# Queue order fixed by a walk over the traced program, and a fourth step by seven products per gate/up group, in a two-layer float32 decoder trunk

## The chip, the cores and the metric

The kernel runs on one core of a Trainium2 chip. The metric is the device time of one execution in microseconds (us). The kernel before takes 1836.91 us, the median of three runs (1836.82 to 1837.41).

## What is computed

The input is one sequence of 256 tokens with 2048 channels in float32, and it passes through two layers. Layer 0 mixes tokens by causal trailing means over windows of 2, 4, 8 and 16 tokens, one window for each quarter of the channels, followed by a 512 x 512 product per quarter. Layer 1 mixes tokens by differential attention with 8 heads. Each layer ends with a SwiGLU feed-forward block of width 5632. A root-mean-square norm stands before every block and at the end.

```python
def diff_attention(h, w_qkv, ...):
    qkv = h @ w_qkv                      # 2048 x 6144
    ...
    a = p[:, :, 0] - lam * p[:, :, 1]    # difference of two softmaxes, head by head
    ...
    return o.reshape(B, S, H * e) @ w_o  # 2048 x 2048

def swiglu(h, wg, wu, wd):               # 2048 x 5632, 2048 x 5632, 5632 x 2048
    return (jax.nn.silu(h @ wg) * (h @ wu)) @ wd

def reference(x, ...):
    h = x
    for i in range(DEPTH):               # DEPTH = 2
        mix = pool_mixer(rmsnorm(h), ...) if i % 2 == 0 else diff_attention(rmsnorm(h), ...)
        h = h + mix
        h = h + swiglu(rmsnorm(h, norm_ffn[i]), w_gate[i], w_up[i], w_down[i])
    return rmsnorm(h, final_norm)
```

## The kernel before

**The products.** Each float32 operand is split into a high and a low part of type float32r (`hi` by a cast, `lo` by subtracting it), and a product is the sum of three matmuls: high by high, high by low, low by high (line 187). The weights are the moving operand, 512 columns wide, and the activations the stationary one, 128 x 128.

`group` (line 147) makes one output block of 256 tokens by 1024 columns. It runs over steps of 256 input channels; a gate/up, q/k, v, o or a full down group has 8 steps. A step's weights come as one load of four blocks of 128 x 512 (`load`, line 116, 1 MiB on the SyncE queue). A step is multiplied in one of two ways:

- plain (line 156): eight block products, two into each of four PSUM banks C11, C12, C21, C22, that is 24 matmuls. It needs `halves` (line 121) of four blocks: a cast on ScalarE (line 124) and a subtraction on VectorE (line 125).
- by seven (line 153): seven block products in the manner of Strassen and Winograd, 21 matmuls, one block product into each of seven banks. It needs sums of the weight blocks (`sums`, line 128, three additions on VectorE at lines 130, 132, 133, written to `tsum`), the halves of these sums (`sum_halves`, line 136: `thi` by a cast on ScalarE at line 139, `tlo` by a subtraction on VectorE at line 140), and the halves of three blocks only.

All eight PSUM banks belong to a group (line 144). Banks 0 to 3 hold M1, M6, M7 and P5, which only steps by seven write; banks 4 to 7 hold P3, P4, M2 and X, which plain steps write under the names C12, C21, C11 and C22. `combined` (line 204) puts the results together with eight additions on VectorE and two copies on ScalarE. Transposes and the attention's small products borrow banks 0 to 3 in turn (`aux`, line 83).

**The stages.** The start (to line 436) loads the tokens and computes layer 0's mixer. `ffn` (line 466) works in chunks of 4, 4 and 3 gate/up groups (`CHUNKS`); each gate/up group gives two `h` tiles through `pair` (line 254), which transposes on TensorE and splits on ScalarE and VectorE; the chunk then runs two down groups with 8, 8 or 6 steps. The attention runs four q/k groups (line 596), each followed by two heads (`head`, line 566, whose scores at line 576, softmax at lines 578 to 592 and transposes at line 561 borrow banks 0 to 3), then two v groups (line 616) and two o groups (line 636).

**Which steps go by seven** is written down in tuples (lines 41 to 47). Gate/up: steps 2, 4, 6, and 4, 6 in the first group of a layer (line 482). Down: 2, 4, 6. The first q/k and the first v group: 4, 6 in natural order. The other q/k and v groups (`LATE`): the order 0, 1, 3, 5, 4, 2, 6, 7, with 4, 2, 6 by seven. An operand for a step by seven is held as eight blocks instead of four (`pair_shape`, line 102).

**Buffers.** Three raw weights (`wraw`), three pairs `whi`, `wlo` (`whl`), one `tsum`; one pair `thi`, `tlo` in the feed-forward blocks, two pairs in q, k, v and o (`bufs=2`).

**What sets the order.** Instructions are traced in the order of the program text. A scheduler of the language then orders each engine's queue from its own cost estimates and priorities; two stretches of the start are given a lower priority (lines 429 and 432). Each engine works through its queue in order and waits on semaphores.

Of the kernel before, what the change touches and what calls it, by code (L numbers as in the profile page):

```python
# [2 lines left out]

# [11 lines left out]
PSUM = bass.MemoryType.PSUM  # L15
# [5 lines left out]
NP = NK // 2  # L21
# [4 lines left out]
EPS = 1e-6  # L26
WARM = 8
LATER = 70

WINDOWS = (2, 4, 8, 16)  # L30

# [6 lines left out]
CHUNKS = (4, 4, 3)  # L38


SEVEN = (2, 4, 6)
SEVEN_DOWN = (2, 4, 6)
SEVEN_QKV = (2, 4, 6)

EARLY = (tuple(range(NP)), (4, 6))
LATE = ((0, 1, 3, 5, 4, 2, 6, 7), SEVEN_QKV)
SEVEN_O = (4, 6)


# [1 line left out]

A22, A21, A11, A12, S1, S3, S2, S4 = range(8)
T1, T3, T2, T4 = range(4)


@with_exitstack
def trunk_kernel(ctx, tc, x_n, gains, scale_in, final_in, subln, lam_in, band, counts_in, dist,
# [408 lines left out]
    def ffn(layer, xq, ss, next_op, next_gain):  # L466
# [3 lines left out]
        with tc.tile_pool(name=f"ffn{layer}", bufs=1, reuse_waits="tile") as hp:  # L470
            g0 = 0
            ys = []
            for c, n in enumerate(CHUNKS):
# [5 lines left out]
                        nc.scalar.dma_start(out=final_sb[i], in_=final_in[:, i * 1024:(i + 1) * 1024])  # L479
                for g in range(g0, g0 + n):  # L480

                    by_seven = SEVEN if g else SEVEN[1:]
                    cs = combined(group([(xq[p], p in by_seven, w_gu[layer][g, p]) for p in range(NP)], hp), hp)
                    for t in range(2):
                        gate, up = cs[t]
                        nc.scalar.activation(gate, gate, AF.Silu, scale=r[:, t:t + 1])
                        nc.vector.scalar_tensor_tensor(up, up, r[:, t:t + 1], gate, ALU.mult, ALU.mult)
                    for i in range(2):
                        at = 2 * (g - g0) + i
                        ht = hp.tile(pair_shape(at in SEVEN_DOWN), F32R, name="h", tag=f"h{at}")  # L490
                        pair(ht, lambda k, t: cs[t][1][:, (2 * i + k) * P:(2 * i + k + 1) * P], None, at in SEVEN_DOWN)
                        hp_tiles.append(ht)
# [35 lines left out]
    with tc.tile_pool(name="attn", bufs=1, reuse_waits="tile") as ap_, ExitStack() as heads:  # L528
# [86 lines left out]
        oT = [None] * NP  # L615
        for g in range(2):
            order, by_seven = LATE if g else EARLY
            cs = scaled(combined(group([(xp[p], p in by_seven, w_v[g, p]) for p in order], op_, bufs=2), op_), (r_col, r_col))
            for h in range(4 * g, 4 * g + 4):
                v = [cs[t][h % 4 // 2][:, h % 2 * E:(h % 2 + 1) * E] for t in range(2)]  # L620
                op = aux((P, 2, E))
# [12 lines left out]
                pair(oT[h], lambda i, t: on[:, t, i * P:(i + 1) * P], [gs[:, i:i + 1] for i in range(2)], h in SEVEN_O)  # L634
        xq = operand(SEVEN)
        for g in range(2):
            cs = combined(group([(oT[p], p in SEVEN_O, w_o[g, p]) for p in range(NP)], op_, bufs=2), op_)
            for b in range(2):
                j = 2 * g + b
                for t in range(2):  # L640
# [2 lines left out]
                transposed(xq, j, 4, SEVEN)  # L643

    ffn(1, xq, ss_next, None, None)


def _steps(w, left, right):
# [85 lines left out]
```

## Time and profile before

| What | Value |
| --- | --- |
| median of three runs | 1836.91 us |
| profiled execution, in all | 1837.09 us |
| its span, first to last instruction | 1835.3 us |
| granted TensorE clock | 0.998 of full speed |
| ScalarE busy | 1048.7 us (57%) |
| memory traffic | 356.35 MB, mean 194 GB/s |
| weight load, issue to landing | 4.8 us median for 1 MiB |

In the profile PE is TensorE's matmuls and PEld its weight loads (which overlap), DVE is VectorE, ACT is ScalarE, SP is SyncE, which issues the large loads. L189 is line 189 of the kernel. `b<-whi,xp` means that a PSUM bank is written from `whi` and `xp`. A group row has the count behind an x, then busy us and the mean ns of one, then the engine's idle time just before these instructions and what ended most of it. A timeline row has the start and the duration in us.

### The profile page before, as it was taken

Reading aid. Unit: us, or ns where it says so; the run is one execution under the profiler, and the core shown is the slowest. Engines: PE = TensorE matmul, PEld = TensorE weight load, DVE = VectorE, ACT = ScalarE, POOL = GpSimd, SP = SyncE. Lnnn points to the kernel's source line nnn. Section 1 sums busy time; section 2 is a strip of 40 time slices with the busy share of each in tenths; the row PEclk is TensorE's granted clock in tenths of the full one; section 3 lists DMA queues with packets and bytes.
Section 4 is the critical chain, followed back from the end, with each engine's and each line's share of the span. In section 5 each row is a group of like instructions: output and inputs, shape, how many; then the busy total and the mean of one; then the engine's idle time right before and its main releaser. Section 6 shows DMA issues by size and latency. Waiting matters only on the chain.

```text
span 1835.3 us, 20926 instructions
## 1 busy us (share of the span) xinstructions
PE 1823.0 (99%) x8192; PEld 1492.3 (81%) x8192; DVE 1630.5 (89%) x1692; ACT 1048.7 (57%) x1026; POOL 0.7 (0%) x6
## 2 busy tenths in 40 slices
PE   9999999999999999999999999999999999999997
PEld 6888888888888888888888888888888888888886
DVE  7999999889899899989988789889899899988986
ACT  6655544555554556666667665555554555555563
POOL 0000000000000000000000000000000000000000
PEclk9999999999999999999999999999999999999999
DMA  7555555555555555544554555555555545556552
GB/s 271 200 184 193 208 196 209 204 187 205 205 194 197 205 184 184 206 173 174 182 183 163 181 184 184 206 185 205 204 190 202 207 183 193 212 215 210 202 189 110
DMA packets 50930, 356.35 MB, mean 194 GB/s; under 512 B 6160, under 2 KB 6288, under 8 KB 8464
## 3 DMA queue, kind: packets, MB, share of 16 engines
q1 hardware_dynamic: 49968, 353.40, 53.5%
q10 hardware_dynamic: 864, 1.63, 0.2%
q8 instruction: 64, 1.05, 0.2%
q14 instruction: 34, 0.28, 0.0%
HBM read 352.90 MB, written 2.10 MB: 193 GB/s over the span
## 4 chain that ended last, share of the span: by engine, by line
PE 97%; DVE 1%; ACT 1%; DMA 0%; issue 0%; SPq 0%; DVEq 0%; ACTq 0%
PE b L189 93%; PE b L259 2%; PE b L576 1%; PE b L607 0%; DMA x_tok<-x_n 0%; PE b L368 0%; PE b L624 0%; PE b L622 0%; PE b L623 0%; PE b L561 0%; DVE wlo L354 0%; DVE xt_hl L252 0%; ACT sq L240 0%; DVE wlo L125 0%; DVE z L392 0%
## 5 line engine op out<-in xcount | busy, mean ns | idle before, releaser
L189 PE MATMUL b<-whi,xp 128*128 128x512 f32 x2784 | 899.4, 392 | 0.0
L124 ACT CAST whi<-raw 128x1536 fp32r<-128x1536 f32 (+1 forms) x328 | 578.7, 1764 | 549.6 <-PE b L189 450.4
L125 DVE TENSOR_TENSOR wlo<-raw,whi 128x1536 fp32r<-128x1536 f32 (+1 forms) x328 | 689.6, 2103 | 159.2 <-ACT whi L124 158.9
L189 PEld LDWEIGHTS b<-whi,xp 128*128 128x128 f32 x2784 | 520.1, 188 | 108.2 <-ACT e L272 0.4
L189 PE MATMUL b<-wlo,xp 128*128 128x512 f32 x1392 | 544.2, 391 | 0.0
L189 PE MATMUL b<-whi,h 128*128 128x512 f32 x1108 | 354.2, 390 | 0.0
L189 PEld LDWEIGHTS b<-wlo,xp 128*128 128x128 f32 x1392 | 261.5, 188 | 53.0
L140 DVE TENSOR_TENSOR tlo<-tsum,thi 128x2048 fp32r<-128x2048 f32 x114 | 260.6, 2286 | 8.3 <-ACT thi L139 8.3
L189 PEld LDWEIGHTS b<-whi,h 128*128 128x128 f32 x1108 | 207.5, 188 | 43.2
L139 ACT CAST thi<-tsum 128x2048 fp32r<-128x2048 f32 x114 | 217.6, 1908 | 19.7 <-DVE tsum L133 17.2
L189 PE MATMUL b<-thi,xp 128*128 128x512 f32 x640 | 223.4, 389 | 0.0
L189 PE MATMUL b<-wlo,h 128*128 128x512 f32 x554 | 215.8, 389 | 0.0
L130 DVE TENSOR_TENSOR tsum<-raw 128x1024 f32<-128x1024 f32 x114 | 139.1, 1220 | 2.1 <-DMA raw<-w_v 0.6
L189 PEld LDWEIGHTS b<-thi,xp 128*128 128x128 f32 x640 | 120.1, 188 | 24.7
L189 PE MATMUL b<-tlo,xp 128*128 128x512 f32 x320 | 125.9, 393 | 0.0
L189 PEld LDWEIGHTS b<-wlo,h 128*128 128x128 f32 x554 | 104.0, 188 | 21.3
L189 PE MATMUL b<-thi,h 128*128 128x512 f32 x240 | 83.7, 390 | 0.0
L133 DVE TENSOR_TENSOR tsum<-tsum,raw 128x512 f32<-128x512 f32 x114 | 78.5, 689 | 2.2
L132 DVE TENSOR_TENSOR tsum<-tsum,raw 128x512 f32<-128x512 f32 x114 | 78.1, 685 | 0.6
L189 PEld LDWEIGHTS b<-tlo,xp 128*128 128x128 f32 x320 | 60.0, 188 | 16.5 <-DVE tlo L140 4.4
L189 PE MATMUL b<-whi,oT 128*128 128x512 f32 x216 | 69.7, 395 | 0.0
L189 PEld LDWEIGHTS b<-thi,h 128*128 128x128 f32 x240 | 45.0, 188 | 9.5 <-ACT thi L139 0.4
(147 smaller groups left out, 1211.7 us busy)
## 6 DMA issues: line engine op xcount, KB each, us to landing
raw<-w_gu SPq DMA_DIRECT2D x176, 1024.0 KB, 4.8
raw<-w_down SPq DMA_DIRECT2D x88, 1024.0 KB, 4.8
raw<-w_qk SPq DMA_DIRECT2D x32, 1024.0 KB, 4.8
raw<-w_v SPq DMA_DIRECT2D x16, 1024.0 KB, 4.8
raw<-w_o SPq DMA_DIRECT2D x16, 1024.0 KB, 4.8
x_tok<-x_n SPq DMA_DIRECT2D x4, 512.0 KB, 6.9
w<-pool_w SPq DMA_DIRECT2D x4, 512.0 KB, 7.5
raw<-pool_w SPq DMA_DIRECT2D x2, 1024.0 KB, 11.1
```

The source lines that it names most:

```text
L124: nc.scalar.copy(hi[:, lo_block:], raw[:, lo_block:])
L125: nc.vector.tensor_tensor(lo[:, lo_block:], raw[:, lo_block:], f32(hi[:, lo_block:]), ALU.subtract)
L130: nc.vector.tensor_tensor(t[:, T1:T3 + 1], raw[:, B11:B22 + 1], raw[:, B12:B12 + 1].broadcast_to([P, 2, 512]), ALU.add)
L132: nc.vector.tensor_tensor(t[:, T2], t[:, T1], raw[:, B22], ALU.add)
L133: nc.vector.tensor_tensor(t[:, T4], t[:, T2], raw[:, B21], ALU.add)
L139: nc.scalar.copy(hi, t)
L140: nc.vector.tensor_tensor(lo, t, f32(hi), ALU.subtract)
L189: nc.tensor.matmul(ps[b], x, y[:, block], start=first, stop=(left[b] == 0))
L259: nc.tensor.transpose(ps[:, i, 1 - t if seven else t], src(i, t), ident)
L576: nc.tensor.matmul(sc[:, :nk], qk[:, 0, c, qb * P:(qb + 1) * P], qk[:, 1, c, :nk], start=True, stop=True)
```

## The change

Two things change together.

1. At the end of the trace a new function, `in_order_of_need`, takes the traced instructions, works out which depends on which (data, buffer slots and PSUM banks), and walks through them: each engine has a fixed time per kind of instruction, and a free engine takes, among the instructions that are able to run, the one of lowest rank. TensorE and the SyncE queue rank by the order of the program text; VectorE and ScalarE rank by when their result is due, reckoned back from TensorE's order. A first walk ranks all by program order; three more follow, and the shortest is kept. The start times of the kept walk then become the queue order of TensorE, VectorE, ScalarE and SyncE, by ordering edges without semaphores.
2. Gate/up groups have four steps by seven, 0, 2, 4, 6; exceptions are layer 0's first group (6 alone), its second (2, 4, 6) and layer 1's first (2, 4, 6). All q/k and v groups take the natural order with 2, 4, 6 by seven. `thi` and `tlo` have one buffer pair in q, k, v and o as well.

The diff, cut where it says "...": left out are some costs of the walk and the reading of dependencies from the trace.

```diff
--- before.py
+++ after.py
@@ -1,3 +1,4 @@
+import heapq
 import math
 from contextlib import ExitStack
 
@@ -26,6 +27,7 @@
 EPS = 1e-6
 WARM = 8
 LATER = 70
+ROUNDS = 3
 
 WINDOWS = (2, 4, 8, 16)
 
@@ -38,12 +40,13 @@
 CHUNKS = (4, 4, 3)
 
 
-SEVEN = (2, 4, 6)
+SEVEN = (0, 2, 4, 6)
 SEVEN_DOWN = (2, 4, 6)
+BEGIN = (((6,), (2, 4, 6)), ((2, 4, 6),))
 SEVEN_QKV = (2, 4, 6)
 
-EARLY = (tuple(range(NP)), (4, 6))
-LATE = ((0, 1, 3, 5, 4, 2, 6, 7), SEVEN_QKV)
+EARLY = (tuple(range(NP)), SEVEN_QKV)
+LATE = (tuple(range(NP)), SEVEN_QKV)
 SEVEN_O = (4, 6)
 
 
@@ -51,6 +54,171 @@
 
 A22, A21, A11, A12, S1, S3, S2, S4 = range(8)
 T1, T3, T2, T4 = range(4)
+
+
+PE, DVE, ACT, SP, POOL = (mybir.EngineType.PE, mybir.EngineType.DVE, mybir.EngineType.Activation,
+                          mybir.EngineType.SP, mybir.EngineType.Pool)
+SIGNAL = 36
+LANDING = 2100
+PER_MIB = 2500
+
+
+class Step:
+
+    def __init__(self, k, ins=None):
+        self.k, self.ins, self.engine = k, ins, ins.engine if ins else POOL
+        self.dma = bool(ins) and ins.opcode == "DMACopy"
+        self.before, self.after = set(), []
+        if not ins:
+            self.holds = self.lasts = 0
+            return
...
+        if self.dma:
+            bytes_ = 4 * math.prod(c for _, c in ins.outs[0].ap)
+            self.share = PER_MIB * bytes_ / 2 ** 20
+            self.holds, self.lasts = (60 if self.engine == ACT else 330), LANDING + self.share
+        elif self.engine == PE:
+            n = size(ins.outs[0])
+            one = 110 if ins.is_transpose else 14 + n / 2.4 if "float32r" in str(ins.ins[0].dtype) else 14 + n / 0.6
+            self.holds, self.lasts = one, one + (0 if ins.is_transpose else 60)
+        elif self.engine == DVE:
+            if ins.opcode == "TensorScalarPtr":
+                self.lasts = 185 + n / 0.96 if n > 8 else 159
+            else:
+                self.lasts = 152 + n / (1.92 if ins.opcode == "TensorCopy" else 0.96)
+            self.holds = max(self.lasts - 80, 60)
...
+
+
+def steps_of(instructions):
+
+    steps, seen, slots, users, gates = [], {}, {}, {}, {}
+    open_, closed, pool_of = [], None, {}
+    for ins in instructions:
...
+        step.before.discard(step.k)
+        steps.append(step)
+    for s in steps:
+        for k in s.before:
+            steps[k].after.append(s.k)
+    return steps
+
+
+def walk(steps, rank):
+
+    missing = [len(s.before) for s in steps]
+    ready, start = [0.0] * len(steps), [0.0] * len(steps)
+    engines = (PE, DVE, ACT, SP, POOL)
+    free, wire = {e: 0.0 for e in engines}, 0.0
+    able, coming = {e: [] for e in engines}, {e: [] for e in engines}
+    for s in steps:
+        if not s.before:
+            heapq.heappush(coming[s.engine], (0.0, s.k))
+    for _ in steps:
+        now, e = min((free[e] if able[e] else max(free[e], coming[e][0][0]), i)
+                     for i, e in enumerate(engines) if able[e] or coming[e])
+        e = engines[e]
+        while coming[e] and coming[e][0][0] <= now:
+            k = heapq.heappop(coming[e])[1]
+            heapq.heappush(able[e], (rank[k], k))
+        s = steps[heapq.heappop(able[e])[1]]
+        start[s.k], free[e] = now, now + s.holds
+        end = now + s.lasts
+        if s.dma:
+            begin = max(now + s.holds, wire)
+            wire = begin + s.share
+            end = begin + s.lasts
+        for k in s.after:
+            same = steps[k].engine == e and not s.dma
+            ready[k] = max(ready[k], now + s.holds if same else end + SIGNAL)
+            missing[k] -= 1
+            if not missing[k]:
+                heapq.heappush(coming[steps[k].engine], (ready[k], k))
+    return start, max(free.values())
+
+
+def due(steps, start):
+
+    by_start = sorted(steps, key=lambda s: start[s.k])
+    at, clock = {}, 0.0
+    for s in by_start:
+        if s.engine == PE:
+            at[s.k], clock = clock, clock + s.holds
+    limit = [0.0] * len(steps)
+    for s in reversed(by_start):
+        limit[s.k] = min([limit[k] - s.lasts - SIGNAL for k in s.after] + [at.get(s.k, clock)])
+    return limit
+
+
+def in_order_of_need(tc):
+
+    steps = steps_of(list(tc.nc.cur_bb.bb.instructions))
+    rank = [float(s.k) for s in steps]
+    start, end = walk(steps, rank)
+    for _ in range(ROUNDS):
+        limit = due(steps, start)
+        rank = [float(s.k) if s.engine in (PE, SP) else limit[s.k] for s in steps]
+        again, span = walk(steps, rank)
+        if span < end:
+            start, end = again, span
+    order = mybir.DependencyInfo(mybir.DependencyClass.NoSync, mybir.DependencyReason.DATA)
+    for e in (PE, DVE, ACT, SP):
+        line = sorted((s for s in steps if s.engine == e), key=lambda s: start[s.k])
+        for one, two in zip(line, line[1:]):
+            tc.add_manual_dep(two.ins, one.ins.name, order, reason="order of need")
+    return start, end, steps
 
 
 @with_exitstack
@@ -479,7 +647,7 @@
                         nc.scalar.dma_start(out=final_sb[i], in_=final_in[:, i * 1024:(i + 1) * 1024])
                 for g in range(g0, g0 + n):
 
-                    by_seven = SEVEN if g else SEVEN[1:]
+                    by_seven = BEGIN[layer][g] if g < len(BEGIN[layer]) else SEVEN
                     cs = combined(group([(xq[p], p in by_seven, w_gu[layer][g, p]) for p in range(NP)], hp), hp)
                     for t in range(2):
                         gate, up = cs[t]
@@ -596,7 +764,7 @@
         for g in range(4):
 
             order, by_seven = LATE if g else EARLY
-            cs = combined(group([(xp[p], p in by_seven, w_qk[g, p]) for p in order], hq, bufs=2), hq)
+            cs = combined(group([(xp[p], p in by_seven, w_qk[g, p]) for p in order], hq, bufs=1), hq)
             cs = scaled(cs, (qs_col, r_col))
             for u in range(2):
                 qk = at.tile([P, 2, 2, S], F32, name="qk")
@@ -615,7 +783,7 @@
         oT = [None] * NP
         for g in range(2):
             order, by_seven = LATE if g else EARLY
-            cs = scaled(combined(group([(xp[p], p in by_seven, w_v[g, p]) for p in order], op_, bufs=2), op_), (r_col, r_col))
+            cs = scaled(combined(group([(xp[p], p in by_seven, w_v[g, p]) for p in order], op_, bufs=1), op_), (r_col, r_col))
             for h in range(4 * g, 4 * g + 4):
                 v = [cs[t][h % 4 // 2][:, h % 2 * E:(h % 2 + 1) * E] for t in range(2)]
                 op = aux((P, 2, E))
@@ -634,7 +802,7 @@
                 pair(oT[h], lambda i, t: on[:, t, i * P:(i + 1) * P], [gs[:, i:i + 1] for i in range(2)], h in SEVEN_O)
         xq = operand(SEVEN)
         for g in range(2):
-            cs = combined(group([(oT[p], p in SEVEN_O, w_o[g, p]) for p in range(NP)], op_, bufs=2), op_)
+            cs = combined(group([(oT[p], p in SEVEN_O, w_o[g, p]) for p in range(NP)], op_, bufs=1), op_)
             for b in range(2):
                 j = 2 * g + b
                 for t in range(2):
@@ -643,6 +811,7 @@
                 transposed(xq, j, 4, SEVEN)
 
     ffn(1, xq, ss_next, None, None)
+    in_order_of_need(tc)
 
 
 def _steps(w, left, right):
```

More of the change, by code (lines that the diff above doesn't have):

```diff
@@ new lines, in steps_of @@
+def steps_of(instructions):
+    steps, seen, slots, users, gates = [], {}, {}, {}, {}
+    open_, closed, pool_of = [], None, {}
+    for ins in instructions:
+        if ins.opcode == "TilePoolBoundary":
+            if ins.op == "release":
+                past = Step(len(steps))
+                past.before = {k for n in seen if pool_of.get(n) == open_[-1] for k in users[n]}
+                past.before |= {closed} if closed is not None else set()
+                closed = past.k
+                steps.append(past)
+                open_.pop()
+                continue
+            open_.append(len(pool_of))
+            pool_of.update((t.name, open_[-1]) for t in ins.bass_pool_tiles or ())
+            continue
+        if not any(hasattr(a, "bass_ap") for a in ins.outs):
+            continue
+        step = Step(len(steps), ins)
+        for writes, args in ((False, ins.ins), (True, ins.outs)):
+            for a in args:
+                ap = getattr(a, "bass_ap", None)
+                if ap is None or not hasattr(ap.tensor, "tag"):
+                    continue
+                t, dims = ap.tensor, [tuple(d) for d in ap.ap]
+                first = ap.offset % dims[0][0]
+                last = first + sum((c - 1) * s for s, c in dims[1:])
+                alone = writes
+                if t.space == PSUM:
+                    first, last, alone = 0, 511, True
+                if t.name not in seen:
+                    seen[t.name], users[t.name], gate = [], [], set()
+                    line = slots.setdefault(t.tag, [])
+                    bufs = t.bufs or t.tag_meta.bufs
+                    if len(line) >= bufs:
+                        gate.update(users[line[-bufs]])
+                    elif t.name in pool_of and closed is not None:
+                        gate.add(closed)
+                    if line:
+                        gate.add(users[line[-1]][0])
+                    line.append(t.name)
+                    gates[t.name] = gate
+                own = {k for f, l, w, k in seen[t.name] if (w or alone) and f <= last and first <= l}
+                step.before |= own or gates[t.name]
+                if alone:
+                    seen[t.name] = [s for s in seen[t.name] if s[0] < first or s[1] > last or s[3] == step.k]
+                seen[t.name].append((first, last, alone, step.k))
+                users[t.name].append(step.k)
+        step.before.discard(step.k)
[4 more added lines that the diff above has]
+    return steps
```

11 lines of the change are left out of this document (added).

## The prediction

> **What bounds the kernel now.** I read the page first, then the chain of waits in order of time, then busy time by windows, then the groups of instructions by form, and last VectorE's timeline in one gate/up group.
>
> ```profile
> PE 1823.0 (99%) x8192; PEld 1492.3 (81%) x8192; DVE 1630.5 (89%) x1692; ACT 1048.7 (57%) x1026; POOL 0.7 (0%) x6
> PE 97%; DVE 1%; ACT 1%; DMA 0%; issue 0%; SPq 0%; DVEq 0%; ACTq 0%
> ```
>
> The chain that ended last is TensorE to 97%, but VectorE is busy 89% of the span. The chain in order of time (start us, us, what) gives the price of one matmul:
>
> ```profile
> 388.88 41.39 PE b L189 x181
> 431.61 41.38 PE b L189 x181
> 474.32 124.36 PE b L189 x547
> ```
>
> 124.36 / 547 = 0.2274 us for each matmul of line 189, with nothing between them over two down groups and what leads up to them. The next view has one row for each stretch: us, then TensorE, weight load, VectorE, ScalarE. The first is a chunk's first gate/up group, the second and third are later ones, the fourth a down group, the fifth a whole chunk of four gate/up and two down groups, and the last two are q/k groups.
>
> ```profile
> 346.42:388.88 42.46, 42.46 (x193) 35.09 (x192) 37.71 (x33) 23.04 (x19) 0.00 (x0) 1.00 0.55 198
> 388.88:431.61 42.73, 42.73 (x193) 35.01 (x192) 38.85 (x36) 24.18 (x21) 0.00 (x0) 1.00 0.56 197
> 431.61:474.32 42.71, 42.71 (x193) 35.01 (x192) 38.85 (x36) 24.17 (x21) 0.00 (x0) 1.00 0.54 197
> 516.70:558.20 41.50, 41.50 (x185) 34.38 (x184) 37.59 (x33) 20.64 (x13) 0.00 (x0) 1.00 0.56 203
> 346.42:600.02 253.60, 253.60 (x1132) 208.83 (x1131) 229.47 (x202) 136.80 (x101) 0.00 (x0) 1.00 0.56 199
> 788.00:836.00 48.00, 48.00 (x226) 39.14 (x225) 44.49 (x68) 30.57 (x42) 0.00 (x0) 1.00 0.49 183
> 836.00:884.00 48.00, 48.00 (x224) 38.46 (x223) 43.83 (x67) 29.93 (x41) 0.00 (x0) 1.00 0.51 176
> ```
>
> In a later gate/up group TensorE never rests and VectorE has 42.71 - 38.85 = 3.86 us to spare. That spare time is what the change spends. What VectorE waits for in it, from the waits of the whole kernel (total us, times, longest):
>
> ```profile
> ACT whi L124 <- PE b L189: 450.4, 206, 4.0
> DVE wlo L125 <- ACT whi L124: 158.9, 131, 3.1
> PEld b L189 <- DVE tlo L140: 6.9, 17, 0.4
> ```
>
> VectorE waits for ScalarE's cast, and the cast waits for TensorE to free one of three weight buffers: VectorE is ahead and held back. The third row shows the few places where TensorE waits for VectorE's `tlo`, 0.4 us each.
>
> **The matmuls removed.** A plain step is 24 matmuls (line 156: eight block products, three each), a step by seven is 21 (line 153). Layer 0's group 0 goes from two sevens to one (+3), its group 1 keeps three, groups 2 to 10 go from three to four (-27). Layer 1's group 0 goes from two to three (-3), its ten others from three to four (-30). In q/k and in v, group 0 goes from two to three (-3 each). Together -63, and 63 x 0.2274 = **-14.3 us** if TensorE stays the bound everywhere. No bytes of DMA change, and the load queue keeps the program's order.
>
> **What 21 more sevens add on VectorE and ScalarE.** By form (count | busy us, mean ns of one | idle before):
>
> ```profile
> L125 DVE TENSOR_TENSOR wlo<-raw,whi 128x2048 fp32r<-128x2048 f32 x214 | 489.8, 2289 | 155.8 <-ACT whi L124 155.8
> L140 DVE TENSOR_TENSOR tlo<-tsum,thi 128x2048 fp32r<-128x2048 f32 x114 | 260.6, 2286 | 8.3 <-ACT thi L139 8.3
> L125 DVE TENSOR_TENSOR wlo<-raw,whi 128x1536 fp32r<-128x1536 f32 x114 | 199.8, 1753 | 3.4 <-ACT whi L124 3.1
> L130 DVE TENSOR_TENSOR tsum<-raw 128x1024 f32<-128x1024 f32 x114 | 139.1, 1220 | 2.1 <-DMA raw<-w_v 0.6
> L133 DVE TENSOR_TENSOR tsum<-tsum,raw 128x512 f32<-128x512 f32 x114 | 78.5, 689 | 2.2
> L132 DVE TENSOR_TENSOR tsum<-tsum,raw 128x512 f32<-128x512 f32 x114 | 78.1, 685 | 0.6
> L124 ACT CAST whi<-raw 128x2048 fp32r<-128x2048 f32 x214 | 409.4, 1913 | 341.2 <-PE b L189 294.9 <-issue 19.2 <-ACT h L263 18.4
> L139 ACT CAST thi<-tsum 128x2048 fp32r<-128x2048 f32 x114 | 217.6, 1908 | 19.7 <-DVE tsum L133 17.2 <-PE b L189 2.5
> L124 ACT CAST whi<-raw 128x1536 fp32r<-128x1536 f32 x114 | 169.3, 1485 | 208.4 <-PE b L189 155.5 <-DVE c L218 33.7 <-issue 17.4
> ```
>
> VectorE: 1.220 + 0.685 + 0.689 + 2.286 + 1.753 - 2.289 = +4.34 us for each step changed. ScalarE: 1.908 + 1.485 - 1.913 = +1.48 us, which a group with 24.17 of 42.71 us busy hides easily; were ScalarE as full as VectorE it would cost those 1.48 us.
>
> How much of 4.34 us VectorE's queue really needs depends on whether its instructions overlap (start us, us):
>
> ```profile
> 449.59 1.23 DVE L130 TENSOR_TENSOR tsum<-raw 128x1024 f32<-128x1024 f32 x1
> 450.74 1.76 DVE L125 TENSOR_TENSOR wlo<-raw,whi 128x1536 fp32r<-128x1536 f32 x1
> 452.42 0.69 DVE L132 TENSOR_TENSOR tsum<-tsum,raw 128x512 f32<-128x512 f32 x1
> 453.13 0.69 DVE L133 TENSOR_TENSOR tsum<-tsum,raw 128x512 f32<-128x512 f32 x1
> ```
>
> `wlo` starts at 450.74, 0.08 us before the end of the instruction ahead of it (450.82); L133, which reads what L132 wrote, starts at 453.13, 0.02 us behind its end. So four more instructions take 4.34 us less 0.08 for each that is not dependent: between 4.0 and 4.4, and I take 4.2.
>
> A later gate/up group with four sevens then asks 38.85 + 4.2 = 43.05 us of VectorE and 42.71 - 3 x 0.2274 = 42.03 us of TensorE. **VectorE is 1.0 us short in each such group.** There are 15 of them: seven in layer 0 (groups 2, 3, 5, 6, 7, 9, 10) and eight in layer 1 (1, 2, 3, 5, 6, 7, 9, 10). A chunk's first group has room (37.71 + 4.2 = 41.9 against 42.46 - 0.68 = 41.8), and a down group leaves VectorE 41.50 - 37.59 = 3.9 us. Over a whole chunk VectorE would need 229.47 + 4 x 4.2 = 246.3 us against TensorE's 253.60 - 2.73 = 250.9: it fits on the average and not group by group.
>
> So the shortfall costs between nothing, if VectorE begins a chunk far enough ahead, and 15 x 1.0 = +15.3 us, if nothing is carried over. How far ahead it can be is set by the buffers: three weights, but one `thi`/`tlo`, so `tlo` of a seven cannot begin before the previous seven is multiplied. The new first step (p = 0) is a seven whose `tlo` falls in the stretch where VectorE also combines the previous group. The trace shows how little is in hand there, at the first seven behind such a stretch in a group of today:
>
> ```profile
> 395.89 2.28 DVE L140 TENSOR_TENSOR tlo<-tsum,thi 128x2048 fp32r<-128x2048 f32 x1
> ...
> 398.23 0.19 PEld L189 LDWEIGHTS b<-tlo,xp 128*128 128x128 f32 x1 [0.42 <-DVE tlo L140]
> ```
>
> With 3.86 us to spare elsewhere in the group, VectorE is still just late here. Against that, the pinned order puts VectorE's and ScalarE's work by when it is due, which this order does not always do. Between the two ends I take the middle: **+7.6 us**.
>
> **The pinned order by itself.** It can give back waits of TensorE, the largest of which are the 6.9 us above. It can lose as much again where the chip runs later than the walk assumed: on an in-order queue the waiting instruction holds all behind it, on VectorE the combine that frees the banks, and then TensorE. I take 0, with -6.9 to +6.9 as ends.
>
> **Natural step order and one `thi`/`tlo` buffer in q, k, v.** Today the sevens of a q/k group come last, so that the previous group's heads use banks 0 to 3 meanwhile (start us, us):
>
> ```profile
> 837.61 0.27 PE L607 MATMUL b<-ident,c 128*128 128x128 f32 x1
> 865.59 0.39 PE L189 MATMUL b<-thi,xp 128*128 128x512 f32 x1
> 866.11 0.44 PE L561 MATMUL b<-ident,a_sb 128*128 128x128 f32 x2
> ```
>
> The heads take 837.61 to 866.55, 28.9 us, and only then come the products with `thi`. In the natural order a seven is third: TensorE has steps 0 and 1 (48), the nine products of step 2 that need none of banks 0 to 3, step 3 (24) and six of step 4, 87 x 0.2274 = 19.8 us, before it must wait. The cost lies between 0 (VectorE does the heads first; it has 4.2 us to spare in the q/k windows) and 4 x (28.9 - 19.8) = +36 us (three q/k groups and v's first). The heads are paced by a queue that had no reason to hurry, so I take +0 and keep the rest as a rival.
>
> The p = 0 operand of both layers also takes the longer form of `pair`, once each:
>
> ```profile
> L252 DVE SCALAR_TENSOR_TENSOR xp<-b,gain_sb,xp 128x256 fp32r<-128x256 f32 x30 | 13.8, 479 | 0.1
> L273 DVE TENSOR_TENSOR e<-e 128x256 f32<-128x256 f32 x27 | 11.3, 419 | 0.4 <-ACT e L272 0.4
> L274 DVE TENSOR_TENSOR e<-e 128x128 f32<-128x128 f32 x27 | 7.7, 284 | 0.0
> L277 DVE TENSOR_TENSOR xp<-e,xp 128x1024 fp32r<-128x1024 f32 x9 | 11.0, 1219 | 0.5 <-ACT xp L276 0.3
> ```
>
> 0.419 + 2 x 0.284 + 1.219 - 2 x 0.479 = +1.25 us of VectorE each, hidden by the products of the group before; without that cover 2.5 us. I cost it at nothing.
>
> **Sum.** -14.3 + 7.6 + 0 + 0 = -6.7 us on the profiled execution's span of 1835.3 us, so 1828.6; that execution took 1837.09 us in all, 1.8 outside the span, and the median is 1836.91. From the median: **1830.2 us**. About 0.2% (3.7 us) is what a measurement here can tell from no change.
>
> **Rivals.**
> One, everything is hidden (chance 0.17): VectorE's lead carries it over each chunk, -14.3 us, **1822.6**. For it: the chunk sums above. Against it: the 0.42 us wait.
> Two, nothing is carried (0.20): each of 15 groups takes VectorE's 43.05 us, -14.3 + 15.3 = +1.0, **1837.9**, no change. For it: the single `tlo` buffer and the seven in first place.
> Three, slower (0.11): VectorE becomes the bound and keeps some of its waits for ScalarE. Today 3.86 us of each group is such waiting; if only 1.0 us survives in each of the 15 groups, +15 more, **1853**. It decides as soon as more than (3.7 - 1.0) / 15 = 0.2 us survives with nothing carried.
> Four, slower through q, k, v (0.09): the heads block banks 0 to 3 as worked out; at half the upper bound, -6.7 + 18 = +11, **1848**.
> Five (0.01): the time follows VectorE's busy time as a whole; 1630.5 + 21 x 4.2 = 1719 at today's share of 88.8% would be 1935 us. The rows speak against it: in three stretches of one chunk TensorE shows no idle time while VectorE does. The Trainium skill, Perfetto Trace Analysis, section Identifying the Most-Contended Engine, holds that TensorE be judged by its weight-load share and VectorE by occupancy; by that rule the 89% of VectorE, not the 81% of the weight loads, is the fullest engine, and work was moved the wrong way. This trace agrees only in so far as VectorE has little left.
> That the ordering edges do not take effect at all would leave today's scheduler with the extra sevens; that is rival two or three.
>
> **How the numbers follow.** Forecast 0.42, rivals 0.17, 0.20, 0.11, 0.09, 0.01. Faster by over 0.2% (below 1833.2): 0.38 of the forecast, all of rival one and 0.02 of rival two, 0.57. Within 0.2%: the other 0.18 of rival two and 0.04 of the forecast, 0.22. Slower: rivals three to five, 0.21. The range runs from below rival one by some recovered waits, 1819, to rival four, 1848, leaving out rival three's centre and beyond.
>
> **What would show it.** Right: 8129 matmuls; VectorE near 1719 us busy; later gate/up groups of 42.0 to 43.0 us with VectorE's idle time under 1 us; down groups at 41.5; TensorE's waits for `tlo` and `wlo` grown to some 8 us. Rival one: groups at 42.0 without such waits. Rivals two and three: groups of 43 us and over, and VectorE the larger part of the chain there. Rival four: q/k groups over 48 us, with waits of TensorE on what lines 563, 578 and 609 (today's numbers) make. I am wrong if down groups or the start change by over 3 us, or if the matmul interval leaves 0.227.

## The result, and the profile after

The changed kernel takes **1864.03 us**, the median of four runs (1863.79 to 1865.86), against 1837.03 before: ratio 1.0149, 95% interval 1.0131 to 1.0166. It is 27.0 us slower where 6.7 us faster was forecast. The profiled execution took 1864.03 us with a span of 1862.2. The change adds lines at the top, so line 189 of before is 357 now, 125 is 293, 140 is 308, 487 (the silu product) is 655 and 259 (the transpose in `pair`) is 427.

From the page of the changed kernel, the busy times and the chain that ended last:

```profile
PE 1819.8 (98%) x8129; PEld 1474.5 (79%) x8129; DVE 1744.2 (94%) x1780; ACT 1081.5 (58%) x1051; POOL 0.7 (0%) x6
PE 49%; DVE 37%; issue 10%; ACT 4%; DVEq 0%; ACTq 0%
```

TensorE was 97% of the chain before and is half of it now; VectorE is 37%. VectorE is busy 114 us longer, where 88 us of work were reckoned. A stretch of four gate/up and two down groups, then one later gate/up group with four sevens by itself (us, then TensorE, weight load, VectorE, ScalarE), and the stretch's longest piece of the chain in order of time:

```profile
389.20:645.76 256.56, 252.69 (x1119) 205.71 (x1119) 248.56 (x218) 141.71 (x104) 0.00 (x0) 1.00 0.54 197
386.48:429.67 43.19, 42.43 (x190) 34.17 (x189) 42.46 (x39) 25.67 (x21) 0.00 (x0) 1.00 0.52 195
```

```profile
478.03 63.30 PE b L357 x279
```

The same work took 253.60 us before. The matmul interval is what it was, 63.30 / 279 = 0.2269 us. So twelve matmuls fewer have been outweighed by 5.7 us in which TensorE waits. In the single group VectorE has 43.19 - 42.46 = 0.7 us left. The waits of the whole kernel tell for what (total us, times, longest; a PEld row counts from the weight load that is held, a PE row only idle TensorE):

```profile
ACT whi L292 <- PE b L357: 377.9, 174, 5.2
DVE wlo L293 <- ACT whi L292: 56.4, 51, 3.1
PEld b L427 <- DVE c L655: 22.0, 32, 1.6
PEld b L357 <- DVE tlo L308: 19.0, 27, 1.6
PE b L427 <- DVE c L655: 10.4, 14, 1.2
PE b L357 <- DVE tlo L308: 9.0, 12, 1.2
```

VectorE's waiting for ScalarE fell from 158.9 to 56.4 us: most of its spare time is gone. The last two rows are new: before, TensorE's waits for `tlo` were 6.9 us of held weight loads, 0.4 us at most, and it had no row for the silu product at all. VectorE's instructions themselves are as long as before (by form):

```profile
L308 DVE TENSOR_TENSOR tlo<-tsum,thi 128x2048 fp32r<-128x2048 f32 x135 | 308.5, 2285 | 2.4 <-ACT thi L307 2.3
L293 DVE TENSOR_TENSOR wlo<-raw,whi 128x2048 fp32r<-128x2048 f32 x193 | 441.3, 2286 | 54.2 <-ACT whi L292 53.9
```

I also added up over all of TensorE's instructions how far each starts behind the one ahead of it beyond the usual distance (0.2268 us for a 512-wide matmul of line 357, 0.110 for a transpose, and so on). This excess is 16.2 us before and 57.4 us after. The difference, 41.2, less 14.3 us of matmuls saved, is 26.9 us, and the spans differ by 26.9. All of the loss is therefore TensorE waiting, and no part of it is slower matmuls. Of the 57.4 us, 14.1 are 22 transposes that wait for the silu product and 12.2 are 19 matmuls that wait for `tlo`; before, no transpose waits so, and the matmuls that wait for `tlo` lose under 0.2 us each. The rest of what is new stands at other transposes, mostly in the attention.

Where the loss lies is told by the first matmul of each stage (us; the last two columns are experiments 1 and 17 below):

| Stage | Before | Changed | Exp. 1 | Exp. 17 |
| --- | --- | --- | --- | --- |
| start | 41.8 | 39.6 | 39.4 | 40.1 |
| feed-forward, layer 0 | 704.5 | 716.2 | 714.8 | 701.6 |
| q, k and v groups | 285.3 | 293.3 | 294.0 | 291.3 |
| o groups | 92.8 | 94.3 | 94.3 | 91.1 |
| feed-forward, layer 1 | 711.0 | 718.8 | 717.4 | 708.4 |

So 19.6 us of the loss are in the two feed-forward blocks and 9.5 in the attention, and the start is 2.2 us shorter.

### The profile page after: what moved, and what is told of

Same layout as the page of the kernel before. It is cut to its first block, busy times and chain, and to the rows that moved or that the text cites. A ratio compares the mean times of both kernels' runs of the same rounds, so it can differ in the third digit from the quotient of the medians.

```text
span 1862.2 us, 20901 instructions
## 1 busy us (share of the span) xinstructions
PE 1819.8 (98%) x8129; PEld 1474.5 (79%) x8129; DVE 1744.2 (94%) x1780; ACT 1081.5 (58%) x1051; POOL 0.7 (0%) x6
## 4 chain that ended last, share of the span: by engine, by line
PE 49%; DVE 37%; issue 10%; ACT 4%; DVEq 0%; ACTq 0%
PE b L357 45%; DVE wlo L293 11%; DVE tlo L308 7%; DVE tsum L298 4%; ACT whi L292 3%; DVE tsum L300 2%; PE b L427 1%; DVE c L381 1%; DVE c L379 1%; DVE c L383 1%; DVE tsum L301 1%; DVE c L380 1%; DVE c L385 1%; DVE c L655 1%; PE b L536 1%
## 5 line engine op out<-in xcount | busy, mean ns | idle before, releaser
L357 PE MATMUL b<-whi,xp 128*128 128x512 f32 x2574 | 839.6, 392 | 0.5 <-DVE c L385 0.5
L293 DVE TENSOR_TENSOR wlo<-raw,whi 128x1536 fp32r<-128x1536 f32 (+1 forms) x328 | 676.5, 2066 | 56.7 <-ACT whi L292 56.4
L357 PEld LDWEIGHTS b<-whi,xp 128*128 128x128 f32 x2574 | 482.8, 188 | 101.8 <-DVE c L385 1.7
L357 PE MATMUL b<-wlo,xp 128*128 128x512 f32 x1287 | 504.3, 392 | 0.0
L308 DVE TENSOR_TENSOR tlo<-tsum,thi 128x2048 fp32r<-128x2048 f32 x135 | 308.5, 2285 | 2.4 <-ACT thi L307 2.3
L307 ACT CAST thi<-tsum 128x2048 fp32r<-128x2048 f32 x135 | 258.0, 1911 | 81.6 <-DVE tsum L301 69.7
L357 PE MATMUL b<-thi,xp 128*128 128x512 f32 x808 | 286.8, 393 | 0.3 <-ACT thi L307 0.3
L357 PEld LDWEIGHTS b<-thi,xp 128*128 128x128 f32 x808 | 151.4, 188 | 34.9 <-DVE h L432 1.7
L357 PE MATMUL b<-tlo,xp 128*128 128x512 f32 x404 | 160.7, 398 | 9.2 <-DVE tlo L308 9.0
L300 DVE TENSOR_TENSOR tsum<-tsum,raw 128x512 f32<-128x512 f32 x135 | 93.3, 691 | 4.0
L301 DVE TENSOR_TENSOR tsum<-tsum,raw 128x512 f32<-128x512 f32 x135 | 93.2, 690 | 3.3
L654 ACT ACTIVATE c<-c,r_tok 128x512 f32<-128x512 f32 x44 | 31.7, 723 | 38.9 <-DVE c L380 24.5
```

The lines of the kernel that those rows point to most:

```text
L293: nc.vector.tensor_tensor(lo[:, lo_block:], raw[:, lo_block:], f32(hi[:, lo_block:]), ALU.subtract)
L300: nc.vector.tensor_tensor(t[:, T2], t[:, T1], raw[:, B22], ALU.add)
L301: nc.vector.tensor_tensor(t[:, T4], t[:, T2], raw[:, B21], ALU.add)
L307: nc.scalar.copy(hi, t)
L308: nc.vector.tensor_tensor(lo, t, f32(hi), ALU.subtract)
L357: nc.tensor.matmul(ps[b], x, y[:, block], start=first, stop=(left[b] == 0))
```

## The experiments

Each edit is made to the changed kernel unless it says otherwise. Five theories were at work: A, the pinned order costs VectorE's time, because dependent instructions stand next to each other; B, the fourth seven fills VectorE and the order is innocent; C, told behind experiment 4, which came out of the first four runs; D, VectorE's load costs, whatever the order; and E, a seven in first place costs, because its `tlo` falls where VectorE combines the group before.

**1. The order alone.** The tuples, step orders and buffers of before, with `in_order_of_need`.

```diff
-SEVEN = (0, 2, 4, 6)
+SEVEN = (2, 4, 6)
-BEGIN = (((6,), (2, 4, 6)), ((2, 4, 6),))
+BEGIN = (((4, 6),), ((4, 6),))
...
```

> The pinned order alone: the sevens, the step order and the buffers of the kernel before. Theory A (the order costs: the walk lets an instruction of VectorE follow at once on one whose result it reads, where the trace shows a loss of about 0.115 us against an independent neighbour; some 40 us of VectorE's time went that way): VectorE's busy time rises by 15 to 30 us over 1630 though no work is added, and the time is 1840 to 1855. Theory B (the load costs: 21 more sevens fill VectorE and the order is innocent): VectorE stays at 1630 and the time is 1830 to 1838.

Measured: 1861.52 us (ratio 1.0133, 1.0118 to 1.0148). The order alone costs 24.5 us with not one instruction of work added; B, which had the order innocent, is out, and the time is above A's range too. Its page, its waits at the silu product, and two stages (layer 0's feed-forward block, then q, k and v) before and here:

```profile
PE 1825.7 (98%) x8192; PEld 1490.6 (80%) x8192; DVE 1658.7 (89%) x1692; ACT 1049.0 (56%) x1028; POOL 0.7 (0%) x6
```

```profile
PEld b L427 <- DVE c L655: 27.4, 43, 1.1
PE b L427 <- DVE c L655: 13.6, 22, 0.7
```

```profile
41.76:746.25 704.49, 704.47 (x3153) 579.10 (x3152) 641.72 (x587) 392.05 (x319) 0.00 (x0) 1.00 0.55 197
746.25:1031.53 285.28, 285.25 (x1324) 231.61 (x1322) 253.64 (x373) 184.01 (x253) 0.00 (x0) 1.00 0.50 178
39.40:754.19 714.79, 706.05 (x3164) 579.56 (x3163) 656.05 (x596) 395.92 (x326) 0.00 (x0) 1.00 0.54 195
754.19:1048.17 293.98, 288.83 (x1319) 231.22 (x1318) 257.77 (x366) 184.35 (x254) 0.00 (x0) 1.00 0.49 175
```

VectorE is busy 28 us longer for the same 1692 instructions, as theory A said: their durations add up to 1740.1 us against 1738.2 before, but they overlap by 81.3 us instead of 107.7. Yet VectorE has idle time left. What holds TensorE in the feed-forward blocks, which take 16.7 us more, is mostly one place, once in each of the 22 gate/up groups; by the count of TensorE's excess these 22 waits are 17.1 us. The attention takes 10.2 us more, with waits of the same kind elsewhere, at the transposes of `a_sb`, of the scaled q and k, and of `o_n`.

**2. The sevens alone**, ordered by the scheduler as before.

```diff
-    in_order_of_need(tc)
```

> The new sevens, step order and buffers alone, the queues ordered as in the kernel before by the language's scheduler. Theory A: VectorE is busy near 1719 us as first worked out, and the time is well under the changed kernel's 1864: 1830 to 1850. Theory B: 1860 or more.

Measured: 1890.50 us (1.0288, 1.0272 to 1.0303), 53.4 us slower. Theory A falls as the whole story: without the pinned order VectorE is busy 1719.9 us, just what the working gave, and it is worse still.

```profile
PEld b L357 <- ACT thi L307: 46.8, 73, 2.2
```

So the two parts do not add: each alone is worse than nothing, +24.5 and +53.4, and together +27.0. With the new sevens the pinned order helps.

**3. The order with three sevens in gate/up**, q, k and v as changed (the first two lines of the diff of experiment 1).

> The pinned order with three sevens per gate/up group as before, but q, k and v as in the changed kernel. Against the order alone it gives the price of the new q, k, v steps, against the changed kernel that of the fourth seven. Theory A: the attention stage is as long as in the changed kernel (about 11 us more than before), the gate/up groups are near 42.7 us. Theory B: under 1840, with the attention stage as before. A third theory (the heads hold banks 0 to 3, rival four of the prediction): the attention stage is 10 us longer than in the order alone.

Measured: 1861.27 us (1.0132, 1.0115 to 1.0148). Against experiment 1 the new q, k, v steps cost nothing (-0.25 us, with six matmuls or 1.4 us fewer). Against the changed kernel the fourth seven costs 2.8 us where 57 x 0.2274 = 13.0 us less matmul time should show: 15.7 us of new waiting. The attention is 9.8 us longer than before here, 10.2 in experiment 1, so the new q, k, v steps don't cause that. None of the three theories had this outcome.

**4. The walk with truer times.** In `walk`, what reads a result on its own engine:

```diff
-            ready[k] = max(ready[k], now + s.holds if same else end + SIGNAL)
+            ready[k] = max(ready[k], (end + (30 if steps[k].engine == DVE else 0) if steps[k].engine in (DVE, ACT) else now + s.holds) if same else end + SIGNAL)
```

> The changed kernel with one line of the walk altered: a dependent instruction on VectorE may start 0.03 us after the end of the one it reads, on ScalarE at its end, instead of 0.08 and 0.03 us before it. Theory A: the walk now puts independent work between dependent instructions, VectorE's busy time falls from 1744 towards 1720 and the time by 10 to 25 us, to 1840 to 1854. Theory B: within 3 us of 1864.

Measured: 1888.93 us (1.0283, 1.0268 to 1.0299). VectorE's busy time did fall, to 1719.4, and the time rose by 25 us, outside the ranges of A and of B. Busy time alone decides nothing here. Theory C: the walk sets TensorE's transposes at the very moment at which it believes the silu product done, and the chip is later there. VectorE's timeline in experiment 1 at the end of a group (start us, us):

```profile
465.95 0.68 DVE L379 TENSOR_TENSOR c<-b,c 128x512 f32<-128x512 f32 x1
466.74 0.69 DVE L381 TENSOR_TENSOR c<-b,c 128x512 f32<-128x512 f32 x1
467.54 0.69 DVE L383 TENSOR_TENSOR c<-c,c 128x512 f32<-128x512 f32 x1
468.26 0.69 DVE L384 TENSOR_TENSOR c<-c,c 128x512 f32<-128x512 f32 x1
468.88 0.68 DVE L380 TENSOR_TENSOR c<-b,c 128x512 f32<-128x512 f32 x1
469.48 2.28 DVE L293 TENSOR_TENSOR wlo<-raw,whi 128x2048 fp32r<-128x2048 f32 x1
471.68 0.68 DVE L385 TENSOR_TENSOR c<-b,c 128x512 f32<-128x512 f32 x1
472.46 0.75 DVE L655 SCALAR_TENSOR_TENSOR c<-c,r_tok,c 128x512 f32<-128x512 f32 x1
```

L380 follows its neighbour after 0.62 us, since it does not need it; the walk reckons 0.605 for all of these. L381 and L655 read the result just ahead, and L383 and L384 overwrite what the one just ahead reads; they follow after 0.79, 0.78, 0.80 and 0.72 us. Together that is 0.67 us late, and of the 22 transposes 21 wait 0.8 us, one 0.5.

**5. Truer times with three sevens** (the edits of 1 and 4).

> The order alone (1861.5) with the walk's dependent instructions on VectorE and ScalarE timed as in the run before. Theory A gave the order alone and the corrected walk each a fall of VectorE's busy time and a gain; with four sevens VectorE's time fell from 1744 to 1719 and the kernel still grew to 1888.9, so busy time is not what the order costs. Theory C (the pinned order sets TensorE's transposes at the very moment the walk believes the silu products done; the chip is 0.6 to 0.8 us later there, since a chain of dependent additions on VectorE runs later than the walk believes, and TensorE waits in its queue: 22 such waits are 17.1 us of the 24.5): the corrected chain moves these transposes back, the waits are gone, 1837 to 1846. Theory A or any other cause: 1855 or more.

Measured: 1846.76 us (1.0052, 1.0036 to 1.0069), 14.8 us better than the order alone. The same stretch now:

```profile
470.54 0.69 DVE L385 TENSOR_TENSOR c<-b,c 128x512 f32<-128x512 f32 x1
471.14 0.68 DVE L386 TENSOR_TENSOR c<-b,c 128x512 f32<-128x512 f32 x1
471.74 0.68 DVE L388 TENSOR_TENSOR c<-b,c 128x512 f32<-128x512 f32 x1
472.33 0.75 DVE L655 SCALAR_TENSOR_TENSOR c<-c,r_tok,c 128x512 f32<-128x512 f32 x1
```

Independent additions stand between L385 and L655, each 0.6 us after the last. The waits for L655 are down from 27.4 to 12.6 us of held weight loads:

```profile
PEld b L427 <- DVE c L655: 12.6, 37, 0.9
```

The time is 0.8 us above C's range. The feed-forward blocks gain 5.2 us of the 14.8 and the attention 9.5, so the silu product is the smaller part of this gain. The edit changes VectorE's order as well as TensorE's. The next three put a margin on TensorE alone, but the walk answers with a new order on the other engines too (in 6 only 844 of VectorE's 1692 instructions keep their place); the run that changes TensorE's order alone is 16.

**6, 7 and 8. Transposes 0.8 us later, and all of TensorE's reads 0.8 us later.**

```diff
+            late = MARGIN if steps[k].engine == PE and steps[k].ins.is_transpose and s.engine in (DVE, ACT) else 0
-            ready[k] = max(ready[k], now + s.holds if same else end + SIGNAL)
+            ready[k] = max(ready[k], now + s.holds if same else end + SIGNAL + late)
```

In 6 on the kernel of experiment 1, in 7 on the changed kernel; in 8 on the changed kernel without the condition on transposes.

> The order alone with one change in the walk: a transpose on TensorE is able to run 0.8 us later than reckoned when it reads what VectorE or ScalarE wrote, so that matmuls that are able already go ahead of it. Nothing else is changed. Theory C: the 17.1 us of waits at the silu products and most of the 8 us of like waits at other transposes go, 1837 to 1845. Against it: the waits move to the next user of banks 0 to 3 or to the h tiles, 1855 or more.

> The changed kernel with the same 0.8 us for transposes. Theory C: the 14.1 us of waits at the silu products and most of the like waits in q, k, v go, the waits for tlo (12.2 us) stay: 1840 to 1850. If the fourth seven alone makes the rest of the loss: 1855 or more.

> The changed kernel with the 0.8 us for every instruction of TensorE that reads or overwrites what VectorE or ScalarE used, so for tlo as well. Theory C: both kinds of waits go, 1825 to 1838, below the kernel before if VectorE has the room that the sum over a chunk gave it (246 of 251 us). If VectorE is simply full: the waits come back elsewhere and the time is that of the run with transposes alone, within 5 us.

Measured: 1851.47 us (1.0078, 1.0063 to 1.0093), 1860.08 us (1.0125, 1.011 to 1.014) and 1853.58 us (1.0089, 1.0074 to 1.0104). All three are better, by 10.0, 4.0 and 10.5 us, and all three miss what theory C gave them. The waits at the silu products are gone in 6 and 7, but new ones stand at `tlo`. These are the rows of 6 (the edit shifts the lines by two: 359 is the product, 310 makes `tlo`):

```profile
PEld b L359 <- DVE tlo L310: 19.8, 31, 1.8
PE b L359 <- DVE tlo L310: 10.7, 12, 1.4
```

**9 and 10. Every seven one step later**, 1, 3, 5, 7, with the pinned order and with the scheduler's.

```diff
-SEVEN = (0, 2, 4, 6)
+SEVEN = (1, 3, 5, 7)
-SEVEN_QKV = (2, 4, 6)
+SEVEN_QKV = (1, 3, 5)
...
```

> The changed kernel with every step by seven one place later: 1, 3, 5, 7 in gate/up groups (7 alone, 3 5 7 and 3 5 7 where it had 6, 2 4 6 and 2 4 6), 1, 3, 5 in q, k, v and 5, 7 in o. As many matmuls, as much work for VectorE. Theory D (load: a gate/up group with four sevens asks more of VectorE than it takes on TensorE): within 4 us of 1864. Theory E (place: a seven in first place needs its tlo while VectorE combines the group before): 1848 to 1856, with the 12.2 us of waits for tlo gone.

> The same places 1, 3, 5, 7, the queues ordered by the language's scheduler. With 0, 2, 4, 6 this took 1890.5. Theory D: within 8 us of 1890. Theory E: 1845 to 1870, since the first step is plain again and TensorE has work while VectorE combines.

Measured: 1877.84 us (1.0222, 1.0204 to 1.0239) and 1933.02 us (1.0519, 1.0503 to 1.0534). Both are outside the ranges of D and of E. In 9 TensorE's idle waits for `tlo` fall from 9.0 to 2.8 us, but with the seven last TensorE waits for the combine, which frees the banks, instead: 9.9 us at L380, and more in 10:

```profile
PE b L357 <- DVE c L380: 31.7, 20, 2.5
```

The shift moves the wait. Whether the first place costs anything by itself is not shown.

**11 and 12. An addition moved to GpSimd**, with the walk as it is and with truer times.

```diff
-        nc.vector.tensor_tensor(t[:, T4], t[:, T2], raw[:, B21], ALU.add)
+        nc.gpsimd.tensor_tensor(t[:, T4], t[:, T2], raw[:, B21], ALU.add)
-            self.holds = self.lasts = 400
+            self.holds = self.lasts = 1000
```

> The changed kernel with the third addition of the weight sums (0.69 us, 135 times) done by GpSimd, which is idle, and counted in the walk at 1.0 us. Takes up to 93 us from VectorE's 1744 us, about 2.8 us from a gate/up group with four sevens. Theory D: 1846 to 1856, the waits for tlo mostly gone, the waits at the silu products left. Theory E: within 5 us of 1864. Against both: GpSimd is so slow, or disturbs VectorE so much, that the time rises.

> The same with the walk's dependent instructions timed as in the corrected walk, which removed most waits at the silu products with three sevens (1861.5 to 1846.8) and made them worse with four (1864 to 1888.9). Theory D: with VectorE relieved the corrected walk behaves as with three sevens, and the fewer matmuls show: 1828 to 1845. If the corrected walk fails for another reason: 1865 or more.

Measured: 1896.67 us (1.0323, 1.0308 to 1.0339) and 2037.60 us (1.109, 1.1074 to 1.1107). Neither tells of load alone. In 11 VectorE was not relieved, 1744.0 us busy with 135 instructions fewer: the addition takes GpSimd 2.47 us in the mean, and VectorE's other instructions grow. In 12 VectorE was relieved, 1677.8 us against 1719.4 in experiment 4, but TensorE waits for `thi`, whose cast now waits for GpSimd. The first two rows are of 11, the third of 12:

```profile
L301 POOL TENSOR_TENSOR tsum<-tsum,raw 128x512 f32<-128x512 f32 x135 | 333.2, 2468 | 1503.0 <-DVE tsum L300 1260.4 <-issue 187.1 <-DVE rs_s L399 34.4
L445 DVE TENSOR_TENSOR h<-e,h 128x1024 fp32r<-128x1024 f32 x16 | 30.5, 1909 | 0.0
PE b L357 <- ACT thi L307: 105.8, 52, 4.8
```

**13, 14 and 15. Less work on VectorE and on no other engine.** The low half of the fourth weight sum is left out, which takes 0.53 us from each seven; 13 on the changed kernel, 14 with the edit of 8, 15 with that of 4.

```diff
-        nc.vector.tensor_tensor(lo, t, f32(hi), ALU.subtract)
+        nc.vector.tensor_tensor(lo[:, :T4], t[:, :T4], f32(hi[:, :T4]), ALU.subtract)
...
+                    at_ = T2 if which and y is lo and block == T4 else block
```

> The changed kernel with less work on VectorE and no other engine used: the low half of the fourth weight sum is left out, so that tlo is 1536 wide instead of 2048, and where it was multiplied the low half of the third sum is used (the matmuls are as many, the result is not the reference's). Takes 135 x 0.53 = 72 us from VectorE, 2.1 us from a gate/up group with four sevens, which was 1.0 us short. Theory D (load): the 12.2 us of waits for tlo go and some of those at the silu products, 1844 to 1853. If the order alone makes the loss: 1858 or more.

> The same with the 0.8 us for all that TensorE reads from VectorE and ScalarE (1853.6 with the full work). If load and the walk's just-in-time order are the two causes and there is no third: TensorE's waits fall to 16 to 30 us, as in the kernel before, and the 63 fewer matmuls show, 1823 to 1840. A third cause: 1845 or more.

> The same left out, with the walk's dependent instructions timed as on the chip (1888.9 with the full work, 1846.8 with three sevens). Theory D: the corrected walk failed with four sevens because it saw VectorE too full, so this falls to 1830 to 1850. If it is the greedy choice of the walk, whatever the load: 1870 or more.

Measured: 1857.01 us (1.0109, 1.0094 to 1.0124), 1833.24 us (0.998, 0.997 to 0.9989) and 1845.84 us (1.0048, 1.0033 to 1.0063). The 65 to 68 us less of VectorE are worth 7.0 us while the just-in-time waits stand, 20.3 us once they are loosened (1853.58 to 1833.24) and 43.1 us with the truer walk (1888.93 to 1845.84). (13 by itself lies between the ranges of the two theories.) So load is a cause, and it is what the truer walk fails on with four sevens. With both causes eased the kernel is below the kernel before, by 0.2% or 3.8 us of the 14.3 that the matmuls save; it leaves out part of the product and is no version to use. The page of 14:

```profile
PE 1814.8 (99%) x8129; PEld 1478.0 (81%) x8129; DVE 1675.6 (91%) x1780; ACT 1079.0 (59%) x1051; POOL 0.7 (0%) x6
```

**16 and 18. TensorE's queue left to the scheduler**, the others pinned; 18 with the edit of 8.

```diff
-    for e in (PE, DVE, ACT, SP):
+    for e in (DVE, ACT, SP):
```

> The changed kernel, full work, with the walk's order for VectorE, ScalarE and the load queue, and TensorE's queue ordered by the language's scheduler around it. Theory C says that TensorE's place for the transposes is what costs 14 us: 1845 to 1856. If VectorE's order is what costs: within 4 us of 1864.

> The changed kernel, full work, with the 0.8 us (1853.6 alone) and with TensorE's queue left to the language's scheduler (1850.0 alone). Both take out the same waits at transposes, so if VectorE's load is all that is left they don't add up: 1847 to 1853. If they remove different waits: 1840 or less.

Measured: 1850.05 us (1.0073, 1.0057 to 1.009) and 1854.81 us (1.0094, 1.0077 to 1.011). In 16 VectorE, ScalarE and the SyncE queue run their instructions in exactly the order of the changed kernel, and VectorE is busy as long (1742.4 us). TensorE's order alone is different, and it is worth 14.0 us at full load; the waits at the silu product are all but gone:

```profile
PEld b L427 <- DVE c L655: 3.0, 10, 0.7
PE b L427 <- DVE c L655: 0.2, 1, 0.2
```

This is the cleanest test of theory C. The margin adds nothing to it: 18 is 4.8 us slower than 16, above the range given for it. With all the work in, no order tried here brings four sevens under 1850 us.

**17. Three sevens, truer times, and all of TensorE's reads 0.4 us later** (the edits of 1, 4 and 8, with 0.4 us).

> Three sevens with the walk's dependent instructions timed as on the chip, which took 1846.8, and 0.4 us later for all that TensorE reads from VectorE and ScalarE. Its waits in that run were of 0.1 to 0.4 us. Theory C with no third cause in the order: the waits go and the order as good as equals the scheduler's, 1834 to 1841. If they come back elsewhere: 1844 or more.

Measured: 1835.21 us (0.9991, 0.9982 to 1.0001), no difference from before that can be told. Its page:

```profile
PE 1815.5 (99%) x8192; PEld 1497.1 (82%) x8192; DVE 1627.7 (89%) x1692; ACT 1049.7 (57%) x1028; POOL 0.7 (0%) x6
```

In total the 24.5 us of the order alone are thus a matter of its timing: corrected and with a margin, the walk's order is as good as the scheduler's, and VectorE's busy time is back at 1628 us. By stage it is a balance: the feed-forward blocks are 5.5 us shorter than before and q, k and v still 6.0 us longer. What those 6.0 us are was not tested; in experiment 5, without the margin, they are 2.1.

## Why the prediction was wrong, step by step

**The matmuls removed** were right: 8129 of them at 0.227 us, -14.3 us, as the excess count confirms.

**The pinned order by itself** is the step that failed. It was put at 0 with ends of -6.9 and +6.9 us, both taken from waits that the trace of before showed; experiment 1 measures +24.5, of which 16.7 are in the feed-forward blocks, 10.2 in the attention and -2.4 in the start. The step named the mechanism (the chip runs later than the walk assumed, and an in-order queue holds all behind) and sized it by the wrong rows. The right rows stood in the prediction: L133 starting 0.02 us behind the L132 that it reads, where the walk lets it start 0.08 us before the end. Four such steps end each gate/up group, and right behind them the walk puts transposes with no slack, in 22 groups. That TensorE's place in the plan costs is shown by experiment 16: 14.0 us with the three other queues in the same order, where the waits at the silu product fall from 14.1 to 0.9 us by the excess count. How the rest divides between VectorE's lost overlap and TensorE's other waits was not separated.

**VectorE's shortfall** was right in kind and stood at its upper end: +7.6 taken, 15.3 as the end, 15.7 measured between experiment 3 and the changed kernel. That one chunk fits (246 of 251 us) did not help, as rival two held. The agreement with 15.3 is partly luck, for the price depends on the order beside it: with the matmuls saved added back, the new sevens cost 22.9 us between experiments 6 and 7, 56.5 between 5 and 4, and 67.7 with the scheduler's order (2), q, k and v included. Its working also missed a part: VectorE is busy 1744 us and not 1719, because dependent neighbours lose their overlap; experiment 1 shows 28 us of the same without a fourth seven. How much of the 15.7 us is this lost overlap and how much the work itself was not separated. One reading was off by a group: the window from 346.42, called a chunk's first gate/up group, is its second, whose first matmul starts at 341.52; the first runs from 300.04 to 341.52, with VectorE busy 37.57 of 41.48 us. The tight groups are then others, but nearly as many.

**Natural order in q, k, v** was put at 0 and cost 1.1 us against its six matmuls. Rival four's cause is out. Its sign came all the same: three of the four q/k groups take over 48 us (50.4, 49.2 and 49.2, from first matmul to first matmul), but in experiment 1, with the step order of before, they take as long (49.9, 49.1 and 49.1). It is the queue order that the attention pays for.

The sum then reads -14.3 + 15.7 + 1.1 + 24.5 = +27.0 us, what was measured; it closes by construction, since each term is the difference of neighbouring runs. Rival three gave the sign and named VectorE, with 1 us of its waits kept in 15 groups; the larger part came instead from TensorE's own queue, at the silu product in all 22 groups and in the attention. Rival five's 1935 us is far off.

Of the signs to look for, the waits for `tlo` came (19.0 us of held weight loads), the count of matmuls and their interval came, and VectorE's 1719 us did not. Later gate/up groups of layer 0 took 43.0 to 43.8 us, which was one half of the sign of rivals two and three; the other half, VectorE as the larger part of the chain, did not come for the whole kernel (37% against 49%). The signs of being wrong (a down group or the start changed by over 3 us, another matmul interval) stayed away: the most are 2.5 us in one down group of layer 0 and 2.2 us in the start.

## What to carry to other kernels

A fixed queue order is only as good as the gap between its planned times and the chip's: check, on the engine that may not wait, how often an instruction is set at the very moment its input is reckoned done, and leave a margin there; here 0.4 us were enough in the feed-forward blocks, together with truer times. Time same-engine dependences apart from independent neighbours before trusting such a plan. Spare time of a second engine, 3.9 us of 42.7 here, makes such errors cheaper to repair: the 0.8 us margin was worth 10.5 us at full load and 23.8 us with less work on VectorE (1857.01 to 1833.24). A saving on the first engine that spends it must be set against the waits that it uncovers. And split a loss by stage before naming its place: the silu product was the plainest wait, and over a third of the order's cost lay in the attention.

## What the hardware showed that I had not expected

GpSimd's addition of 128x512 float32 takes 2.47 us in the mean of experiment 11, 1.28 at the least, where VectorE needs 0.69. While it runs, some of VectorE's instructions are slowed: a subtraction of 128x1024 took 1.91 us against 1.22. Of the 273 that overlap such an addition 86 are over 0.1 us longer than in the changed kernel, and the growth is 86.1 us in all; the 1372 others did not grow. VectorE's total stayed at 1744 us. The Trainium skill, Perfetto Trace Analysis, section Optimizing Scalar/DVE Operations, warns that moving work between these two might not help because they share a read port; this case agrees: in experiment 11 the move gave back nearly all of the 93 us that it took, in experiment 12 some 39 us. That the port is the reason is the page's word; no run here shows it.

The two parts of one change had opposite signs in company: the pinned order costs 24.5 us with the sevens of before and gains 26.5 us (1890.50 to 1864.03) with the new ones.
